# HGRN2 keys as logarithms, clamped sigmoids, one modulation vector fewer, and a plan with more trials, in a two-layer hybrid backbone

## The chip, the cores and the metric

The kernel runs on 1 core of one Trainium2 chip. The metric is the device time of one execution in microseconds (us). The engines of the core run side by side and wait for one another through semaphores: TensorE (PE, matmuls), VectorE (DVE), ScalarE (ACT), GpSimd (POOL) and SyncE (SP, which starts the DMAs here).

## The reference

Two layers work on 256 latent and 256 context tokens of width 1024. What matters here is the HGRN2 mixer, a gated linear recurrence run in both directions over 8 heads of 128 keys, and the modulation that scales and shifts the normalized tokens:

```python
def hgrn2_direction(q, i, z, lb, s0):
    f = lb + (1.0 - lb) * jax.nn.sigmoid(z)
    log_f = jnp.log(jnp.maximum(f, HG_MIN_F))
    k = (1.0 - lb) * jax.nn.sigmoid(-z)
    return hgrn2_chunk_scan(q, k, i, log_f, s0)

# in hgrn2_chunk_scan, per chunk:
    cum = jnp.cumsum(fb, axis=2)
    o_inter = einsum(qb * jnp.exp(cum), state)
    diff = cum[:, :, :, None, :] - cum[:, :, None, :, :]
    scores = einsum('bhtk,bhsk,bhtsk->bhts', qb, kb, exp(diff) where s <= t)
    new_state = state * exp(last) + einsum(kb * jnp.exp(last - cum), vb)

# in reference, per layer:
    need_ctx = l < DEPTH - 1
    sh1, sc1, ga1, sh2, sc2, ga2 = adaln_modulation(c, ...)
    csh1, csc1, cga1, csh2, csc2, cga2 = adaln_modulation(c_ctx, ...)
```

Beside HGRN2 run attention and a long convolution (Hyena); the three are merged with sigmoid gates, projected, and an MLP follows. In layer 1 (the last) the context tokens are only read by the mixers: of their modulation, nothing but the first shift and scale is used. The lower bound `lb` is zero in layer 0.

## The kernel before

All tokens are held with channels on the 128 partitions, 512 tokens (256 latent, 256 context) along the free axis. Every weight block of 128 x 1024 is one *job* in `run_jobs`: a DMA brings `raw`, ACT casts it to `whi`, DVE (for a few blocks POOL) subtracts to get `wlo`, and PE runs three matmuls for each of eight blocks of the inner dimension (high times high and the two cross terms), into the PSUM tile `pd`. A function given with the job then takes the result out of PSUM. In layer 0 most jobs have 512 columns; in layer 1, `q`, the gates, the branches and the MLP have 256.

The HGRN2 jobs of a layer (`hgrn_jobs`) come first. Per head they are the two gate projections `z` (one for each direction), `q` and the output gate, with `v` projected for two heads at a time. `hg_z` turns a `z` of 512 columns into the key `k` and the logarithm of the forget gate `ls`, with `softplus_parts` as its first step: Abs, Exp and Ln on ACT, and min-and-subtract on DVE. `softplus_parts` also serves the output gate (`ev_g`) and the merge gates (`sigmoid`). `hg_scan` then works on one head:

- two prefix sums `cf`, `cb` on DVE;
- per direction the keys decayed to the end of their chunk, `kh`: a subtraction on POOL, an Exp on ACT, a product with `k` on DVE, then transposes (`kt`) and state updates (`pu`, `st`) on PE;
- for four block sizes h = 64, 32, 16, 8 the decayed queries `dq` and keys `dk`: four subtractions on POOL, two Exps on ACT, on DVE one product for `dq` and two half-width products for `dk`, then small matmuls into the scores `sc`;
- inside blocks of 8 the same with `dp`, `dm`; the diagonal with `kd`; then the output `po`, its norm and the gate.

The modulation of layer 1, and part of layer 0's, is worked out on DVE by `ada_vec`: per chunk of 128 channels a DMA of 128 x 1024 (`adav`, in a slot of the `raw` pool), and for each of the two vectors (latent, context) one multiply-and-sum `junk` over 1024 columns. These chunks run as fillers: 40 chunks of layer 1 beside the MLP of layer 0, 8 beside the MLP of layer 1.

The order of all instructions is fixed ahead by a planner. `Plan.record` notes each operation with a cost from `Plan.cost`, its inputs and its priority; `Plan.schedule` simulates five in-order engines and the tile slots (a ring of 63 tiles of 512 columns, 4 `raw`, 4 `whi`, 4 `wlo`, 8 PSUM banks) and picks, for each engine, what can start first. An operation that feeds another engine is assumed to be seen there 60 ns after its end, and 1400 ns (`TLAT`) after it if the other is PE. Between two operations of one engine nothing is added. `Plan.issue` writes the instructions out in that order, so that all of them carry line 433.

Of the kernel before, what the change touches and what calls it, by code (L numbers as in the profile page):

```python
# [22 lines left out]
P = 128  # L23
# [8 lines left out]
MIN_F = 1e-6  # L32
ATT_SCALE = P ** -0.5
# [22 lines left out]
TLAT = 1400.0  # L56
# [91 lines left out]
class Op:  # L148
    __slots__ = ("eng", "calls", "cost", "prio", "succ", "soft", "ndep", "ready", "allocs", "uses", "start", "fin", "seq", "lat", "tail", "lock")
# [7 lines left out]
class Plan:  # L157
# [13 lines left out]
    def cost(self, eng, m, outs, ins, kw):  # L171
# [3 lines left out]
        if eng == "tensor":  # L175
# [3 lines left out]
            if o.shape[0] <= 64:  # L179
                return (45.0 if o.shape[0] > 32 else 50.0 if n >= 128 else 14.0), 165.0, False  # L180
# [35 lines left out]
    def record(self, eng, calls):  # L216
# [9 lines left out]
        for m, a, kw in calls:  # L226
# [4 lines left out]
            c, op.tail, lock = self.cost(eng, m, outs, ins, kw)  # L231
            op.cost += c
# [6 lines left out]
        soft = set()  # L239
        for vt, c in list(rd) + list(wr):  # L240
# [38 lines left out]
    def schedule(self, caps, margin, window):  # L279
        SEM = 60.0  # L280
        lat = {(a, b): 60.0 for a in ENGS for b in ENGS}
        for e in ENGS:
            lat[e, "tensor"] = TLAT
# [44 lines left out]
        while len(order) < total:  # L328
# [127 lines left out]
class Kern:  # L456
# [284 lines left out]
    def ada_vec(self, l, c0, c1):  # L741
        nc = self.nc
        for ch in range(c0, c1):
# [3 lines left out]
            m = self.modb[l][ch // 16][:, ch % 16, :]  # L747
            for v in range(2):
# [1071 lines left out]
```

## Time and profile before

| what | value |
|---|---|
| median of 3 runs | 2187.66 us (2187.34 to 2192.6) |
| the profiled execution | 2191.69 us |
| its span, first to last instruction | 2189.9 us |
| PE busy | 2105.6 us (96%) |
| DVE busy | 1836.8 us (84%) |
| ACT busy | 1201.1 us (55%) |
| POOL busy | 812.8 us (37%) |
| mean granted TensorE clock | 0.984 |

The first layer's HGRN2 lies between about 90 and 430 us, its other mixers and merge up to about 980, its MLP up to about 1300; the second layer's HGRN2 between about 1380 and 1680 us, then its other mixers to about 1850, then merge and MLP. A busy PE is one that has a matmul under way: matmuls overlap, and their ends are modelled. The granted clock is a mean over a stretch of TensorE's two levels, 1.2 GHz (0.5) and 2.4 GHz (1.0).

### The profile page before, as it was taken

What the parts mean: (1) busy time and instruction counts of PE and PEld (TensorE: products, weight loads), DVE (VectorE), ACT (ScalarE), POOL (GpSimd) and SP (SyncE); (2) the same over time, 40 slices, a digit from 0 to 9 for tenths busy, and PEclk for the clock granted to TensorE, in tenths of its full rate; (3) what the DMA queues carried; (4) which work ended last, traced back from release to release, by engine and by line L of the source; (5) the groups of instructions that cost most, each with busy time, mean ns of one, the idle gap of its engine ahead of it and who ended that gap; (6) DMA issues with size and microseconds to landing.
All of it is one profiled execution on the core that took longest, in us unless ns stands there. A gap on an engine that the chain in (4) does not pass through costs nothing.

```text
span 2189.9 us, 38470 instructions
## 1 busy us (share of the span) xinstructions
PE 2105.6 (96%) x14721; PEld 1863.7 (85%) x14721; DVE 1836.8 (84%) x2940; ACT 1201.1 (55%) x2192; POOL 812.8 (37%) x894
## 2 busy tenths in 40 slices
PE   6999999999999999999999989999888999999999
PEld 3888887888888888889888878888778998999999
DVE  8889999998887777788888887899888999668776
ACT  5667757533477534455332334768675458576553
POOL 3565656655430123153100113554645762112110
PEclk9899999999999999999999999999998999999999
DMA  9422222323221454454666654422224433667665
GB/s 331 135 73 78 71 85 69 107 78 97 85 73 52 144 153 154 145 204 128 203 192 194 190 174 154 135 88 78 78 78 154 155 103 95 184 187 211 219 223 154
DMA packets 105608, 301.63 MB, mean 138 GB/s; under 512 B 11456, under 2 KB 26832, under 8 KB 105296
## 3 DMA queue, kind: packets, MB, share of 16 engines
q1 hardware_dynamic: 105424, 299.17, 43.7%
q8 instruction: 116, 1.90, 0.4%
q14 instruction: 68, 0.56, 0.1%
HBM read 281.82 MB, written 14.69 MB: 135 GB/s over the span
## 4 chain that ended last, share of the span: by engine, by line
PE 53%; DVE 27%; DMA 7%; issue 6%; ACT 4%; POOL 2%; SPq 0%; DVEq 0%; POOLq 0%; ACTq 0%
PE pd L433 41%; DMA adav<-in_ada_t 6%; DVE wlo L433 6%; PE pdt L433 4%; DVE junk L433 3%; DVE dk L433 2%; DVE sp L433 1%; ACT sp L433 1%; PE py L433 1%; DVE dq L433 1%; ACT whi L433 1%; PE att L433 1%; PE px L433 1%; DVE hyu L433 1%; DVE mx L433 1%
## 5 line engine op out<-in xcount | busy, mean ns | idle before, releaser
L433 PE MATMUL pd<-hhi,wlo 128*128 128x512 f32 (+2 forms) x1984 | 697.2, 351 | 10.3 <-DVE wlo L433 6.9
L433 PE MATMUL pd<-hlo,whi 128*128 128x512 f32 (+2 forms) x1984 | 683.5, 344 | 0.4 <-DVE hlo L433 0.3
L433 PE MATMUL pd<-hhi,whi 128*128 128x512 f32 (+2 forms) x1984 | 683.4, 344 | 0.0
L433 ACT CAST whi<-raw 128x1024 fp32r<-128x1024 f32 x392 | 409.8, 1047 | 366.8 <-PE pd L433 319.3
L433 DVE TENSOR_TENSOR wlo<-raw,whi 128x1024 fp32r<-128x1024 f32 x376 | 508.8, 1357 | 90.7 <-ACT whi L433 89.8
L433 PEld LDWEIGHTS pd<-hhi,wlo 128*128 128x128 f32 x1984 | 380.8, 192 | 54.3 <-DVE wlo L433 7.1
L433 PEld LDWEIGHTS pd<-hlo,whi 128*128 128x128 f32 x1984 | 380.4, 192 | 45.5 <-DVE hlo L433 1.1
L433 PEld LDWEIGHTS pd<-hhi,whi 128*128 128x128 f32 x1984 | 381.2, 192 | 39.4
L433 DVE SCALAR_TENSOR_TENSOR junk<-adav,crowb 128x1024 bf16<-128x1024 f32 x160 | 205.2, 1299 | 89.4 <-DMA adav<-in_ada_t 87.3
L433 ACT ACTIVATE sp<-sp 128x512 f32<-128x512 f32 (+1 forms) x288 | 160.7, 560 | 71.0 <-DVE sp L433 64.9
L433 POOL TENSOR_TENSOR glo<-relu,ghi 128x512 fp32r<-128x512 f32 (+1 forms) x32 | 46.1, 1440 | 354.2 <-ACT ghi L433 297.7
L433 PE MATMUL pd<-ghi,wlo 128*128 128x256 f32 (+1 forms) x528 | 175.4, 332 | 0.0
L433 PE MATMUL pd<-glo,whi 128*128 128x256 f32 (+1 forms) x528 | 174.9, 331 | 0.0
L433 PE MATMUL pd<-ghi,whi 128*128 128x256 f32 (+1 forms) x528 | 174.8, 331 | 0.0
L433 PE MATMUL pd<-ahi,wlo 128*128 128x512 f32 (+1 forms) x384 | 129.0, 336 | 0.0
L433 PE MATMUL pd<-alo,whi 128*128 128x512 f32 (+1 forms) x384 | 129.0, 336 | 0.0
L433 PE MATMUL pd<-ahi,whi 128*128 128x512 f32 (+1 forms) x384 | 128.9, 336 | 0.0
L433 POOL TENSOR_TENSOR sp<-sp,sp 128x512 f32<-128x512 f32 (+1 forms) x32 | 40.5, 1266 | 208.5 <-DVE sp L433 208.5
L433 PEld LDWEIGHTS pd<-ghi,whi 128*128 128x128 f32 x528 | 100.2, 190 | 9.4
L433 PEld LDWEIGHTS pd<-glo,whi 128*128 128x128 f32 x528 | 100.2, 190 | 9.4
L433 PEld LDWEIGHTS pd<-ghi,wlo 128*128 128x128 f32 x528 | 100.3, 190 | 9.3
L433 ACT CAST ghi<-relu 128x512 fp32r<-128x512 f32 (+1 forms) x64 | 32.9, 514 | 130.9 <-DVE relu L433 126.3
(301 smaller groups left out, 4569.5 us busy)
## 6 DMA issues: line engine op xcount, KB each, us to landing
raw<-in_w_in SPq DMA_DIRECT2D x180, 512.0 KB, 3.7
raw<-in_w_mlp SPq DMA_DIRECT2D x128, 512.0 KB, 4.3
adav<-in_ada_t SPq DMA_DIRECT2D x80, 512.0 KB, 4.2
raw<-in_w_branch SPq DMA_DIRECT2D x48, 512.0 KB, 3.7
raw<-in_w_tm SPq DMA_DIRECT2D x20, 512.0 KB, 3.7
hd<-fhs SPq DMA_DIRECT2D x32, 256.0 KB, 4.0
hf<-hd SPq DMA_DIRECT2D x32, 256.0 KB, 4.8
raw<-in_w_out SPq DMA_DIRECT2D x16, 512.0 KB, 3.7
```

The source lines that it names most:

```text
L433: getattr(eng, m)(*[res(v) for v in a], **{k: res(v) for k, v in kw.items()})
```

## The change

1. *Sigmoids.* `softplus_parts` goes. A new `clamp` bounds `z` to plus or minus 44 on DVE, reading PSUM, and `softplus` makes ln(1 + exp(sign z)) with Exp and Ln on ACT. `hg_z` calls it twice: `lf` is minus the logarithm of sigmoid(z), `nk` minus that of sigmoid(-z). `k` is one Exp of `nk`, in layer 1 with the logarithm of 1 - lb (`lolb`, made once) as the bias. The merge and output gates use the same two functions.
2. *Keys as logarithms.* `hg_scan` makes, for each direction, `g` = prefix sum minus the key's logarithm, on DVE, in the tile of `nk`. The decayed keys `kh` and `dk` are then one exponential of a difference with `g`: for `kh` three activations of 128 columns with a bias (`eb`, a tiny DVE product) in place of a POOL subtraction, one activation and a DVE product; for `dk` the same POOL subtractions and activation, and no DVE product.
3. *Context modulation.* In layer 1 `ada_vec` makes only the latent vector for chunks 16 to 47.
4. *The plan.* Reading what the same engine (other than PE and SP) has just written waits until its end and 40 ns more. Small matmuls cost other amounts, and 186 or 380 ns are added for the first of a group. The assumed latencies to PE (800 to 2600 ns) and to the others (60, 100, 150 ns) are tried in fifteen pairs, and the order that ends first by the planner's own count is taken.

```diff
-TLAT = 1400.0
+TRIALS = [(t, e) for t in (800.0, 1100.0, 1400.0, 1700.0, 2600.0) for e in (60.0, 100.0, 150.0)]
...
             if o.shape[0] <= 64:
-                return (45.0 if o.shape[0] > 32 else 50.0 if n >= 128 else 14.0), 165.0, False
+                return (52.0 if o.shape[0] > 32 else 19.4 if n <= 32 else 12.0 + 0.42 * n), 165.0, False
...
+            if eng == "tensor" and m == "matmul" and outs[0].shape[0] <= 64 and not op.cost:
+                c += 380.0 if outs[0].shape[0] > 32 else 186.0
...
+        op.reads = {vt.writer[c] for vt, c in rd if vt.writer[c] is not None and vt.writer[c].eng == eng}
...
+        found = [(attempt(x)[0], i) for i, x in enumerate(trials)]
+        return attempt(trials[min(found)[1]])[1]
...
-                x.ready = max(x.ready, free_t[e] if x.eng == e and not o.lat else o.fin + lat[e, x.eng])
+                if x.eng != e or o.lat:
+                    t = o.fin + lat[e, x.eng]
+                else:
+                    t = o.fin + RAW if o in x.reads and e not in ("tensor", "sync") else free_t[e]
+                x.ready = max(x.ready, t)
...
+            nv = 1 if l == DEPTH - 1 and ch >= 16 else 2
+            m = self.modb[l][ch // 16][:, ch % 16, 0:nv]
-            for v in range(2):
+            for v in range(nv):
...
-    def softplus_parts(self, z, n):
+    def clamp(self, z, n):
+        t = self.T("zc")[:, :n]
+        self.nc.vector.tensor_scalar(out=t, in0=z, scalar1=-ZCAP, scalar2=ZCAP, op0=ALU.max, op1=ALU.min)
+        return t
+
+    def softplus(self, z, n, sign):
         nc = self.nc
         t = self.T("sp")[:, :n]
-        nc.scalar.activation(out=t, in_=z, func=AF.Abs)
-        nc.scalar.activation(out=t, in_=t, func=AF.Exp, scale=-1.0)
+        nc.scalar.activation(out=t, in_=z, func=AF.Exp, scale=sign)
         nc.scalar.activation(out=t, in_=t, func=AF.Ln, bias=1.0)
-        nc.vector.scalar_tensor_tensor(out=t, in0=z, scalar=0.0, in1=t, op0=ALU.min, op1=ALU.subtract)
         return t
...
     def hg_z(self, l, dr, hd, z):
-        ls = self.softplus_parts(z, 512)
+        z = self.clamp(z, 512)
+        lf = self.softplus(z, 512, -1.0)
+        nk = self.softplus(z, 512, 1.0)
         k = self.T("hk")
-        nc.vector.tensor_tensor(out=k, in0=ls, in1=z, op=ALU.subtract)
-        nc.scalar.activation(out=k, in_=k, func=AF.Exp)
         if l == 0:
-            nc.vector.tensor_scalar(out=ls, in0=ls, scalar1=math.log(MIN_F), scalar2=None, op0=ALU.max)
+            nc.scalar.activation(out=k, in_=nk, func=AF.Exp, scale=-1.0)
+            nc.vector.tensor_scalar(out=lf, in0=lf, scalar1=-math.log(MIN_F), scalar2=None, op0=ALU.min)
         else:
...
+            nc.scalar.activation(out=k, in_=nk, func=AF.Exp, scale=-1.0, bias=self.lolb[:, i:i + 1])
...
-            nc.vector.tensor_scalar(out=k, in0=k, scalar1=self.olb[:, i:i + 1], scalar2=None, op0=ALU.mult)
-        return k, ls
+        return k, lf, nk
...
+        gf, gb = nkf, nkb
+        for d, (g_, c_) in enumerate(((gf, cf), (gb, cb))):
+            if l == 0:
+                V.tensor_tensor(out=g_, in0=c_, in1=g_, op=ALU.subtract)
+            else:
+                i = d * 8 + hd
+                V.scalar_tensor_tensor(out=g_, in0=g_, scalar=self.lolb[:, i:i + 1], in1=c_, op0=ALU.subtract, op1=ALU.add)
...
-            e = ch(c_)[:, :, last:last + 1]
-            G.tensor_tensor(out=ch(kh), in0=ch(c_), in1=e.to_broadcast([P, 4, P]), op=ALU.subtract)
-            A.activation(out=kh, in_=kh, func=AF.Exp, scale=-1.0)
-            V.tensor_tensor(out=kh, in0=kh, in1=k_, op=ALU.mult)
+            e = ch(c_)[:, :, last:last + 1].rearrange("p c o -> p (c o)")
...
+            el = self.S([P, 4], "eb")
+            V.tensor_scalar(out=el, in0=e, scalar1=sg, scalar2=None, op0=ALU.mult)
+            for c in order:
+                sl = slice(c * P, (c + 1) * P)
+                A.activation(out=kh[:, sl], in_=g_[:, sl], func=AF.Exp, scale=-sg, bias=el[:, c:c + 1])
...
-            G.tensor_tensor(out=bl(dk)[:, :, :h], in0=cfb[:, :, :h], in1=rf, op=ALU.subtract)
-            G.tensor_tensor(out=bl(dk)[:, :, h:], in0=cbb[:, :, h:], in1=rb, op=ALU.subtract)
+            G.tensor_tensor(out=bl(dk)[:, :, :h], in0=bl(gf)[:, :, :h], in1=rf, op=ALU.subtract)
+            G.tensor_tensor(out=bl(dk)[:, :, h:], in0=bl(gb)[:, :, h:], in1=rb, op=ALU.subtract)
...
-            V.tensor_tensor(out=bl(dk)[:, :, :h], in0=bl(dk)[:, :, :h], in1=bl(kf)[:, :, :h], op=ALU.mult)
-            V.tensor_tensor(out=bl(dk)[:, :, h:], in0=bl(dk)[:, :, h:], in1=bl(kb)[:, :, h:], op=ALU.mult)
...
-        order = self.plan.schedule(CAPS, MARGIN, WINDOW)
+        order = self.plan.best_schedule(CAPS, MARGIN, WINDOW, TRIALS)
```

## Rows read from the trace of the kernel before

**Rows 1.** The page: span, and busy us of each engine.
```profile
span 2189.9 us, 38470 instructions
PE 2105.6 (96%) x14721; PEld 1863.7 (85%) x14721; DVE 1836.8 (84%) x2940; ACT 1201.1 (55%) x2192; POOL 812.8 (37%) x894
```

**Rows 2.** Busy time by stretch: length, engines' busy us, clock, DMA share, GB/s.
```profile
0.00:100.00 100.00, 77.41 (x518) 61.30 (x519) 88.55 (x176) 56.62 (x104) 43.48 (x40) 0.91 0.67 237
100.00:450.00 350.00, 341.11 (x3161) 286.96 (x3160) 325.11 (x447) 229.94 (x415) 213.01 (x243) 1.00 0.27 82
...
700.00:1300.00 600.00, 599.64 (x2838) 504.06 (x2837) 474.90 (x714) 243.43 (x363) 117.61 (x83) 1.00 0.54 169
1300.00:1380.00 80.00, 71.64 (x396) 62.10 (x395) 63.54 (x93) 37.85 (x63) 34.03 (x31) 0.96 0.42 135
1380.00:1700.00 320.00, 286.79 (x2553) 261.39 (x2552) 282.50 (x490) 215.28 (x470) 172.83 (x262) 0.94 0.34 105
1700.00:1850.00 150.00, 144.31 (x1068) 136.58 (x1068) 142.00 (x253) 92.93 (x197) 78.43 (x74) 0.99 0.38 115
1850.00:2189.90 339.90, 335.60 (x2776) 334.24 (x2774) 245.83 (x399) 191.49 (x322) 53.80 (x50) 1.00 0.64 194
```

**Rows 3.** PE's waits, 1380 to 1700 us: total us, times, longest.
```profile
PE sc L433 <- DVE dm L433: 13.5, 6, 4.8
PE pd L433 <- DVE wlo L433: 5.9, 4, 2.4
PE po L433 <- DVE am L433: 4.3, 1, 4.3
PE kt L433 <- DVE kh L433: 3.5, 1, 3.5
```

**Rows 4.** DVE's groups by form: shapes, count, busy us, mean ns, idle before.
```profile
L433 DVE SCALAR_TENSOR_TENSOR junk<-adav,crowb 128x1024 bf16<-128x1024 f32 x160 | 205.2, 1299 | 89.4 <-DMA adav<-in_ada_t 87.3 <-issue 2.1
L433 DVE SCALAR_TENSOR_TENSOR sp<-pd,sp 128x512 f32<-128x512 f32 x64 | 43.8, 685 | 12.1 <-ACT sp L433 11.9
L433 DVE TENSOR_TENSOR dk<-dk,hk 128x256 f32<-128x256 f32 x64 | 40.0, 665 | 2.5 <-ACT dk L433 2.4
L433 DVE TENSOR_TENSOR kh<-kh,hk 128x512 f32<-128x512 f32 x32 | 28.0, 886 | 1.0 <-ACT kh L433 0.8
L433 DVE TENSOR_TENSOR dk<-dk,hk 128x128 f32<-128x128 f32 x64 | 25.3, 429 | 1.8 <-ACT dk L433 1.6
L433 DVE TENSOR_TENSOR hk<-sp,pd 128x512 f32<-128x512 f32 x32 | 21.9, 686 | 0.9
L433 DVE TENSOR_SCALAR sp<-sp 128x512 f32<-128x512 f32 x32 | 17.3, 541 | 0.9
L433 DVE TENSOR_SCALAR hk<-hk,olb 128x512 f32<-128x512 f32 x16 | 9.1, 566 | 1.2 <-ACT hk L433 1.2
L433 DVE TENSOR_SCALAR mx<-mx 128x1 f32<-128x1 f32 x48 | 7.0, 151 | 1.0
```

**Rows 5.** ACT's groups by form.
```profile
L433 ACT ACTIVATE sp<-sp 128x512 f32<-128x512 f32 x192 | 120.8, 631 | 59.0 <-DVE sp L433 55.1
L433 ACT ACTIVATE sp<-sp 128x256 f32<-128x256 f32 x96 | 40.1, 418 | 12.0 <-DVE sp L433 9.8
L433 ACT ACTIVATE sp<-pd 128x512 f32<-128x512 f32 x64 | 37.7, 589 | 4.3 <-PE pd L433 4.1
L433 ACT ACTIVATE relu<-relu,w1b 128x256 f32<-128x256 f32 x32 | 16.2, 507 | 3.2 <-DVE relu L433 3.1
```

**Rows 6.** POOL's groups by form: the removed subtraction, one of its two kinds.
```profile
L433 POOL TENSOR_TENSOR kh<-cf 128x512 f32<-128x512 f32 x16 | 23.1, 1444 | 16.8 <-DVE cf L433 16.8
```

**Rows 7.** DVE's groups, 1400 to 1700 us: the weights' low part.
```profile
L433 DVE TENSOR_TENSOR wlo<-raw,whi 128x1024 fp32r<-128x1024 f32 x39 | 57.7, 1483 | 6.4 <-ACT whi L433 6.0
```

**Rows 8.** DVE's timeline, 1604 to 1640 us: start, us, instruction.
```profile
1609.96 4.22 DVE L433 TENSOR_TENSOR wlo<-raw,whi 128x1024 fp32r<-128x1024 f32 x1
...
1633.46 1.21 DVE L433 TENSOR_TENSOR wlo<-raw,whi 128x1024 fp32r<-128x1024 f32 x1
```

More of the change, by code (lines that the diff above doesn't have):

```diff
@@ L148 @@
 class Op:
-    __slots__ = ("eng", "calls", "cost", "prio", "succ", "soft", "ndep", "ready", "allocs", "uses", "start", "fin", "seq", "lat", "tail", "lock")
+    __slots__ = ("eng", "calls", "cost", "prio", "succ", "soft", "ndep", "ready", "allocs", "uses", "start", "fin", "seq", "lat", "tail", "lock", "reads")
 ENGS = ("tensor", "vector", "scalar", "gpsimd", "sync")
@@ L277, in record, with best_schedule, attempt, schedule @@
         return op
-    def schedule(self, caps, margin, window):
-        SEM = 60.0
-        lat = {(a, b): 60.0 for a in ENGS for b in ENGS}
+    def best_schedule(self, caps, margin, window, trials):
+        ndep = [o.ndep for o in self.ops]
+        vts = list({id(v): (v, v.left) for o in self.ops for v in o.uses}.values())
+        def attempt(x):
+            for o, n in zip(self.ops, ndep):
+                o.ndep, o.ready = n, 0.0
+            for v, n in vts:
+                v.left, v.slot, v.end = n, None, 0.0
+            try:
+                order = self.schedule(caps, margin, window, *x)
+            except RuntimeError:
+                return 1e12, None
+            return max(o.fin for o in order), order
+        found = [(attempt(x)[0], i) for i, x in enumerate(trials)]
+        return attempt(trials[min(found)[1]])[1]
+    def schedule(self, caps, margin, window, tlat, elat):
+        SEM, RAW = 60.0, 40.0
+        lat = {(a, b): elat for a in ENGS for b in ENGS}
         for e in ENGS:
-            lat[e, "tensor"] = TLAT
+            lat[e, "tensor"] = tlat
         lock_t, lock_e = 0.0, None
@@ L754, in ada_vec @@
                 if chunk <= ch < chunk + 8:
-                    nc.vector.tensor_scalar(out=self.amod[l][which][:, ch - chunk, :], in0=m, scalar1=1.0,
+                    nc.vector.tensor_scalar(out=self.amod[l][which][:, ch - chunk, 0:nv], in0=m, scalar1=1.0,
                                             scalar2=self.pv(g, l * 8 + ch - chunk), op0=ALU.add, op1=ALU.mult)
@@ L1223, in hg_scan @@
         for c_ in (cf, cb):
-            A.activation(out=c_[:, :nq], in_=c_[:, :nq], func=AF.Exp)
+            A.activation(out=c_[:, :nq], in_=c_[:, :nq], func=AF.Exp, scale=sg)
             V.tensor_tensor(out=c_[:, :nq], in0=c_[:, :nq], in1=q[:, :nq], op=ALU.mult)
@@ L1263, in ev_z @@
                     s = st[hd]
[L1264 removed]
+                    d = "fb"[dr]
+                    s["k" + d], s["l" + d], s["nk" + d] = self.hg_z(l, dr, hd, z)
                 def ev_q(z, hd=hd):
@@ L1271, in ev_g @@
                 def ev_g(z, hd=hd):
-                    t = self.softplus_parts(z, nq)
-                    nc.scalar.activation(out=t, in_=t, func=AF.Exp)
+                    t = self.sigmoid(z, nq)
                     nc.vector.tensor_tensor(out=t, in0=t, in1=z, op=ALU.mult)
@@ L1493, in sigmoid @@
     def sigmoid(self, z, n):
-        t = self.softplus_parts(z, n)
-        self.nc.scalar.activation(out=t, in_=t, func=AF.Exp)
+        t = self.softplus(self.clamp(z, n), n, -1.0)
+        self.nc.scalar.activation(out=t, in_=t, func=AF.Exp, scale=-1.0)
         return t
```

34 lines of the change are left out of this document (19 added, 15 removed).

## The prediction

> **What bounds the kernel now.** Read the page from the top. TensorE (PE) is busy for 96% of the span, VectorE (DVE) for 84% [rows 1]. A PE that is busy all the time can't be helped by work taken from DVE, so the next question is where the missing 4% lies, and the view that answers it is the busy time by stretch [rows 2]. From 700 to 1300 us PE is busy 599.64 of 600 us: there TensorE alone sets the time, and nothing that the change does to other engines can shorten it; its matmuls are the same before and after. The same holds from 1850 us on, where 335.60 of 339.90 us are busy and the rest is the tail.
>
> The loss is in four other stretches, and the granted clock belongs to it: in 1380 to 1700 us PE is idle for 320 - 286.8 = 33.2 us, and the clock is 0.94 on average, so that of the two levels, 1.2 and 2.4 GHz, it spent about 12% at the lower one, worth up to 0.06 x 320 = 19.2 us of full-speed work. Together 52.4 us. The same sum gives 11.6 us for 1300 to 1380 (8.4 idle, 3.2 clock), 7.2 us for 1700 to 1850 (5.7 and 1.5), and 8.9 us, all of it idle, for 100 to 450 us [rows 2]. That is 80.1 us which the change could reach at most; it is an upper bound, since idle time and low clock overlap in part. The first 100 us lose 31.6 us more (22.6 idle, 9 clock), but in start-up work that the change hardly touches.
>
> 1380 to 1700 us is the HGRN2 mixer of the second layer. There DVE is busy 282.5 of 320 us (88%), while ScalarE (ACT) has 215.3 and GpSimd (POOL) 172.8 [rows 2], and the waits of PE name DVE: the scores' matmuls wait 13.5 us for `dm`, the projections 5.9 us for `wlo` [rows 3]. So in this stretch DVE's queue is what ends last. The first layer's mixer (100 to 450) has DVE at 325.1 of 350 us, and yet PE at 97.5%: its jobs are 512 columns wide, so PE has more to do for the same DVE work. These two stretches are where the change removes DVE work.
>
> **Part by part: DVE.** Durations are means of one instruction in the profiled execution.
> - *Sigmoid parts* (`hg_z`). Before, each of 16 calls per layer made on DVE the min-and-subtract from PSUM (685 ns), `k = ls - z` (686), the bound on the logarithm (541), and in layer 1 also scaling and `k` times `olb` (566) [rows 4]. After, a clamp reading PSUM takes the place of the first, and `k` comes from ACT alone. The trace has no clamp; the rows bound it by 541 ns (a two-scalar operation from SBUF) and 685 (a PSUM read of the same width), and I take 685, as it reads PSUM. So 0.69 us less per call in layer 0, 11 us in all, and 0.69 + 0.57 = 1.25 us less in layer 1, 20 us in all.
> - *Scan.* Per head two `kh` products (886 each) go, and eight `dk` products (665 each at 256 columns in layer 0, 429 each at 128 in layer 1). Added are two operations `g = c - nk` with two SBUF inputs over 512 columns, for which I take the 886 of `kh`, and two tiny scalings (151, the row of `mx`) [rows 4]. Layer 0: 1.77 + 5.32 - 1.77 - 0.30 = 5.0 us a head, 40 us for eight. Layer 1: 1.77 + 3.43 - 1.77 - 0.30 = 3.1 us, 25 us for eight.
> - *Modulation of context.* 32 of layer 1's 48 chunks lose one of two `junk` products of 1.30 us [rows 4]: 24 before 1300 us (31 us of DVE), 8 in the last MLP (10 us).
>
> So DVE falls by about 51 us of 325 in the first mixer, by 45 us of 282 in the second, by 31 us ahead of 1300 us. The last lies where PE is full, so by itself it is hidden at no gain; it can only let the filter units and the normalization at 1300 us come earlier.
>
> **POOL and ACT.** POOL loses two `kh` subtractions a head, 1.44 us each [rows 6]: some 20 us of its 173 in the second mixer. This helps DVE twice over, since DVE's times there swing with what runs beside it: one `wlo` took 4.22 us and another 1.21 us [rows 8]. The 39 `wlo` of this stage average 1.48 us [rows 7], 0.27 above that 1.21, 11 us in all beside 173 us of POOL work; an eighth of POOL's work goes, so 1.3 us, and as `wlo` is a fifth of DVE's time here I count four times that, 5 us; bounds 0 and 20 us (all of POOL's time).
>
> ACT gains work. Each `hg_z` has one activation more (631 instead of an Abs at 589 plus 631 new: 0.67 us), so 10.7 us per layer. `kh` becomes three activations of 128 columns with a bias from memory in place of one of 512 at about 0.63 us. From 631 at 512 and 418 at 256 columns the fixed part is 205 ns, so 128 columns cost 311; a pointer adds 507 - 418 = 89; together 400 each, 1.2 us for three, at most 0.57 more per `kh`, and 9 us for the sixteen of a layer. The output gate's sigmoid gives back one activation a head (5 us and 3 us) [rows 5]. ACT in the second mixer goes from 215 to about 232 us, still beside DVE's work. The last `eb` and `el` operations are on the path of `kh`, but a POOL pass of 1.4 us and a DVE product go out of the same path, so it gets shorter.
>
> A rule of the Trainium skill (ScalarE: Activation LUTs, What ACT_TABLE_LOAD costs) speaks against that split: it gives an activation with a pointer bias 280 ns + 0.833 ns per column, an immediate one 186 ns + 0.833 ns, and an overlap of 93 ns back to back. By it, as an estimate, three pieces cost 3 x 294 = 881 ns of throughput against 520, or 5.8 us per layer instead of my 9. Rows 5 agree with the pointer's price (89 ns against 93). The sum by it would be 3 us of ACT time smaller, which changes no term on the path.
>
> **The new plan.** Three things change in the order itself: a wait of 40 ns behind each read-after-write on one engine, dearer small matmuls, and fifteen trials of assumed latencies, of which the one that finishes first by its own arithmetic is taken. The trace of before can't show that order. Its bounds from the rows: at best PE gets all of the 80 us back; at worst the first mixer loses PE time at the rate at which the second does now, 350 x (0.104 + 0.06) - 8.9 = +48 us [rows 2]. I take zero for the order itself, because the other mixer's 2.5% loss shows that an order with long assumed PE latency already hides nearly everything when DVE keeps up.
>
> **The sum.** Second mixer: DVE needs 282.5 - 45 - 5 = 232 us, while PE needs 320 - 52 = 268. DVE's share would be 87%, below the 93% with which the first mixer lost 2.5%. So most of the 52.4 us should come back; I take 40, since the jobs here are short and waits on single heads stay. First mixer: 5 of 8.9. 1300 to 1380: 6 of 11.6, from the 31 us of DVE that go ahead of it. 1700 to 1850: 3 of 7.2, since the attention there is not touched. Start: 0. Together 54 us. The profiled execution took 2191.69 us (span 2189.9, 1.8 around it); it would become 2137.7. The median of the three timed runs is 2187.66, 4 us lower, and gives 2134.
>
> **The rivals.**
> 1. *ACT takes DVE's place.* With 232 us of ACT work and in-order queues, a stage of 270 us has ACT at 86% and DVE at 86%. Two full queues that wait on each other (`sp`, `hk` go back and forth) lose more than one. For it: ACT is the engine that grows. Against it: ACT idles a third of that stage now. It would return half, 27 us: 2161.
> 2. *All of the loss returns.* Shorter waits also keep the clock at its upper level, which has cost up to 19 us in the second mixer; then 80 us come back: 2108.
> 3. *PE's loss is not DVE's work but the heads' dependence.* The single-head chain of scan, exponentials, scores and output ends late whatever DVE's load is. Then only the shorter path of `kh` pays: 1.44 + 0.89 - 0.89 - 0.57 = 0.9 us per pass, of which PE waited for 3.5 us in the second mixer [rows 3]: 2184, no change that a measurement can tell. Against it: that stage's DVE is never idle for long.
> 4. *The plan turns against it.* The trial chosen by its own finish favours short assumed latencies, since the latency is part of that finish. PE's order is fixed; with operands planned closer, it stands in front of late ones in both mixers. From the point on where the first mixer's loss grows by more than the second one's gain the kernel is slower. At the second mixer's present rate in the first (+48) and nothing gained in the second: 2236; half of it: 2212.
> 5. *More live tiles.* Two more 512-column tiles live per head from the projection to the scores, in a ring of 63. If the ring runs out, allocation holds back the next head. I put it with rival 1, as it has the same place and size.
>
> **Chances.** Forecast (2120 to 2160) 0.50; rival 1 and 5 (2160 to 2181) 0.20; rival 2 (below 2120) 0.12; rival 3 0.08; rival 4 0.10. About 0.3%, 6.6 us, is what a measurement of this kernel can tell from no change; so faster 0.82, same 0.08, slower 0.10. Range 2100 to 2180: it takes in rival 1 and nearly all of rival 2, and leaves out rivals 3 and 4, 0.18.
>
> **What would show it.** Right: in the stretch between the second layer's first and last HGRN2 projections PE idles under 15 us, its clock stays at 0.98 or more, and DVE's busy time falls by some 45 us there; the waits of the scores on `dm` shrink; the stretch of 600 us of full PE keeps its length. DVE's sum over the span should be about 140 us lower, POOL's 45 lower, ACT's within 20 us of before. Wrong: DVE falls so, and PE's idle time doesn't, with ACT or a single head's chain at the end of its waits (rivals 1, 3), or PE idles in the first mixer where it did not (rival 4).

## The result, and the profile after

| what | before | after |
|---|---|---|
| median | 2187.5 us (2185.86 to 2192.6) | 2123.89 us (2121.76 to 2124.91) |
| the profiled execution | 2191.69 us | 2123.79 us |
| its span | 2189.9 us | 2121.6 us |

The ratio after to before is 0.9706, with a 95% interval of 0.969 to 0.9722: 63.6 us less. The forecast was 2134, in a range of 2100 to 2180.

The head of the page, which answers [rows 1]: span, then busy time, share of the span and instructions of each engine; below it the granted clock in 40 slices, and the shares of the chain that ended last.

```profile
span 2121.6 us, 38292 instructions
PE 2085.7 (98%) x14721; PEld 1847.3 (87%) x14721; DVE 1674.8 (79%) x2733; ACT 1187.6 (56%) x2225; POOL 785.0 (37%) x862
PEclk9999999999999999999999999999999999999999
PE 85%; DVE 8%; ACT 4%; DMA 1%; issue 1%; SPq 0%; POOL 0%; ACTq 0%; DVEq 0%
```

DVE lost 162 us, POOL 28, ACT 13.5. PE's idle time fell from 84.3 us (2189.9 - 2105.6) to 35.9 (2121.6 - 2085.7). That is 48.4 of the 68.3 us by which the profiled span is shorter; the other 19.9 are PE's own busy time for the same 14721 matmuls, and the mean granted clock went from 0.984 to 0.996. The chain that ended last is PE for 85% of the span.

To see where the time went, the two traces must be cut at the same work, since the second mixer of after begins 24 us earlier. The cuts here are the starts of the same projection matmuls (the n-th of the program in both). Busy time by stretch, columns as in [rows 2]; first the stretches of before that [rows 2] cuts elsewhere:

```profile
0.00:80.00 80.00, 57.41 (x374) 42.46 (x375) 70.61 (x140) 42.98 (x77) 37.89 (x37) 0.89 0.73 262
80.00:450.10 370.10, 361.21 (x3305) 305.90 (x3305) 343.14 (x483) 243.58 (x441) 218.70 (x247) 1.00 0.28 85
450.10:980.30 530.20, 529.31 (x2688) 449.88 (x2686) 423.71 (x669) 269.21 (x466) 170.98 (x161) 1.00 0.39 120
980.30:1300.10 319.80, 319.44 (x1574) 271.27 (x1574) 265.57 (x421) 107.78 (x158) 46.20 (x37) 1.00 0.58 181
...
1700.00:2189.90 489.90, 479.90 (x3842) 470.82 (x3841) 387.83 (x650) 284.41 (x518) 132.23 (x124) 1.00 0.56 170
```

and then the same work in after, all seven stretches:

```profile
0.00:70.50 70.50, 53.33 (x349) 36.50 (x350) 59.31 (x130) 38.10 (x68) 33.95 (x35) 0.93 0.78 284
70.50:445.90 375.40, 374.33 (x3437) 320.18 (x3435) 311.78 (x460) 257.78 (x502) 220.93 (x254) 1.00 0.29 89
445.90:962.20 516.30, 516.30 (x2585) 438.18 (x2582) 399.10 (x639) 249.55 (x434) 153.50 (x139) 1.00 0.39 121
962.20:1283.00 320.80, 319.90 (x1575) 271.21 (x1575) 248.26 (x385) 113.51 (x166) 59.19 (x42) 1.00 0.59 186
1283.00:1355.60 72.60, 70.67 (x404) 61.87 (x403) 54.68 (x82) 34.52 (x58) 30.61 (x28) 1.00 0.45 149
1355.60:1643.50 287.90, 282.10 (x2620) 257.75 (x2619) 236.56 (x427) 222.64 (x517) 166.20 (x254) 0.99 0.36 115
1643.50:2121.60 478.10, 469.10 (x3766) 461.56 (x3764) 365.09 (x616) 271.51 (x486) 120.66 (x113) 1.00 0.55 171
```

The second mixer (320 us in [rows 2], 287.9 here) gave 32.1 us, the start 9.5, the first mixer with what follows it 8.6 (5.3 longer and 13.9 shorter: 132 matmuls more lie in the former, 103 fewer in the latter), 1300 to 1380 gave 7.3 and the rest 11.8. The cuts don't part PE's work quite the same way: 25 matmuls fewer lie in the start, 67 more in the second mixer, 76 fewer behind it. So neighbouring stretches are best read together. The 320 us of full PE from 980 on kept their length (+1.0). In the second mixer PE idles 5.8 us instead of 33.2, at a clock of 0.99 instead of 0.94, with 45.9 us less of DVE. PE's waits there (total us, times, longest), to be set beside [rows 3]:

```profile
PE pd L460 <- DVE wlo L460: 2.9, 1, 2.9
PE pu L460 <- ACT kts L460: 1.3, 2, 0.7
PE pdt L460 <- ACT hhi L460: 0.7, 1, 0.7
PE oss L460 <- POOL csl L460: 0.4, 1, 0.4
PE kt L460 <- ACT kh L460: 0.2, 1, 0.2
```

The 13.5 us for `dm` are gone, and so are those for `am` and for `kh` of DVE. What ACT took over is hardly waited for: 2.2 us in all.

The new instructions, by form (count, busy us, mean ns, idle before), beside [rows 4] and [rows 5]:

```profile
L460 DVE TENSOR_SCALAR zc<-pd 128x512 f32<-128x512 f32 x64 | 43.7, 683 | 21.8 <-PE pd L460 21.4
...
L460 DVE TENSOR_SCALAR eb<-cb 128x4 f32<-128x4 f32 x16 | 10.5, 658 | 0.0
...
L460 DVE SCALAR_TENSOR_TENSOR sp<-sp,lolb,cb 128x512 f32<-128x512 f32 x8 | 8.2, 1025 | 0.0
...
L460 DVE TENSOR_TENSOR sp<-cb,sp 128x512 f32<-128x512 f32 x8 | 6.1, 757 | 0.4
...
L460 DVE TENSOR_SCALAR eb<-cf 128x4 f32<-128x4 f32 x16 | 5.0, 315 | 0.0
...
L460 ACT ACTIVATE kh<-sp,eb 128x128 f32<-128x128 f32 x96 | 33.1, 392 | 27.0 <-DVE eb L460 26.8
...
L460 ACT ACTIVATE hk<-sp,lolb 128x512 f32<-128x512 f32 x16 | 11.4, 715 | 0.0
L460 ACT ACTIVATE hk<-sp 128x512 f32<-128x512 f32 x16 | 10.1, 631 | 0.3
```

### The profile page after: what moved, and what is told of

Read it like the earlier page. It is cut to its first block, busy times and chain, and to the rows that moved or that the text cites. A ratio compares the mean times of both kernels' runs of the same rounds, so it can differ in the third digit from the quotient of the medians.

```text
span 2121.6 us, 38292 instructions
## 1 busy us (share of the span) xinstructions
PE 2085.7 (98%) x14721; PEld 1847.3 (87%) x14721; DVE 1674.8 (79%) x2733; ACT 1187.6 (56%) x2225; POOL 785.0 (37%) x862
## 4 chain that ended last, share of the span: by engine, by line
PE 85%; DVE 8%; ACT 4%; DMA 1%; issue 1%; SPq 0%; POOL 0%; ACTq 0%; DVEq 0%
PE pd L460 68%; PE pdt L460 4%; PE py L460 2%; PE px L460 1%; DVE wlo L460 1%; PE sco L460 1%; PE att L460 1%; PE sc L460 1%; PE po L460 1%; ACT sp L460 1%; DVE y L460 1%; PE pu L460 1%; PE ptr L460 1%; ACT whi L460 1%; DVE hlo L460 1%
## 5 line engine op out<-in xcount | busy, mean ns | idle before, releaser
L460 ACT CAST whi<-raw 128x1024 fp32r<-128x1024 f32 x392 | 410.8, 1049 | 540.1 <-PE pd L460 487.9
L460 PE MATMUL pd<-hhi,wlo 128*128 128x512 f32 (+2 forms) x1984 | 689.8, 348 | 4.5 <-DVE wlo L460 4.5
L460 DVE TENSOR_TENSOR wlo<-raw,whi 128x1024 fp32r<-128x1024 f32 x376 | 499.1, 1329 | 104.1 <-ACT whi L460 103.0
L460 PEld LDWEIGHTS pd<-hhi,whi 128*128 128x128 f32 x1984 | 376.9, 190 | 39.2
L460 DVE SCALAR_TENSOR_TENSOR junk<-adav,crowb 128x1024 bf16<-128x1024 f32 x128 | 165.4, 1310 | 76.8 <-DMA adav<-in_ada_t 76.7
L460 ACT ACTIVATE sp<-sp 128x512 f32<-128x512 f32 (+1 forms) x224 | 122.4, 566 | 3.0 <-DVE sp L460 0.7
L460 POOL TENSOR_TENSOR pa<-pa,pb 128x256 f32<-128x256 f32 x96 | 79.7, 863 | 76.8 <-DVE pb L460 69.5
```

The costliest lines, as they stand in the source:

```text
L460: getattr(eng, m)(*[res(v) for v in a], **{k: res(v) for k, v in kw.items()})
```

## The experiments

Ratios are to the kernel before, timed beside each on the same chip; "against after" is the difference of the two ratios times 2187.5 us.

| kernel | what it is | median us | ratio [95%] | against after |
|---|---|---|---|---|
| after | | 2123.89 | 0.9706 [0.969, 0.9722] | |
| e1_plan_only | arithmetic of before, new plan | 2173.85 | 0.9929 [0.9912, 0.9945] | +48.8 |
| e2_math_only | arithmetic of after, old plan | 2147.60 | 0.9808 [0.9793, 0.9822] | +22.3 |
| e3_ctx_back | both modulation vectors | 2131.97 | 0.9736 [0.9721, 0.9751] | +6.6 |
| e4_keys_back | keys as products | 2153.83 | 0.9836 [0.9822, 0.9851] | +28.4 |
| e5_dve_load | 8 products more a head | 2136.23 | 0.9764 [0.975, 0.9779] | +12.7 |
| e6_old_costs | old costs of small matmuls | 2135.28 | 0.9758 [0.9743, 0.9772] | +11.4 |
| e7_no_raw | no same-engine wait | 2127.52 | 0.9723 [0.9708, 0.9738] | +3.7 |
| e8_1700_60 | one fixed pair of latencies | 2122.02 | 0.9699 [0.9683, 0.9715] | -1.5 |
| e9_dve_pool_load | e5 and 2 POOL passes a head | 2152.20 | 0.9835 [0.9821, 0.985] | +28.2 |
| e10_trials_only | only the trials of the new plan | 2136.42 | 0.9755 [0.9737, 0.9772] | +10.7 |
| e11_wide_trials | 48 other pairs | 2134.56 | 0.9751 [0.9735, 0.9768] | +9.8 |
| e12_sigm_back | old sigmoid parts | 2122.64 | 0.9697 [0.9682, 0.9711] | -2.0 |

Lengths of the seven stretches, in us, cut at the same matmuls in the profile of each kernel (4 of the 12 in full, the others where they are used):

| kernel | start | first mixer | to 980 | to 1300 | to 1380 | second mixer | rest |
|---|---|---|---|---|---|---|---|
| before | 80.0 | 370.1 | 530.2 | 319.8 | 79.9 | 320.0 | 489.9 |
| after | 70.4 | 375.4 | 516.3 | 320.8 | 72.7 | 287.9 | 478.1 |
| e1_plan_only | 69.4 | 388.4 | 522.4 | 321.1 | 77.1 | 306.7 | 485.3 |
| e2_math_only | 79.6 | 369.3 | 518.2 | 319.9 | 69.1 | 304.4 | 485.9 |
| e4_keys_back | 70.5 | 387.7 | 523.7 | 320.5 | 72.5 | 292.3 | 484.8 |
| e9_dve_pool_load | 70.2 | 378.2 | 526.2 | 320.0 | 72.5 | 299.7 | 483.2 |

**Plan or arithmetic.** The theory was that the arithmetic brings nearly everything and the order nothing. Two kernels each take one half.

e1_plan_only, before with the planner of after:

```diff
-TLAT = 1400.0
+TRIALS = [(t, e) for t in (800.0, 1100.0, 1400.0, 1700.0, 2600.0) for e in (60.0, 100.0, 150.0)]
...
-        order = self.plan.schedule(CAPS, MARGIN, WINDOW)
+        order = self.plan.best_schedule(CAPS, MARGIN, WINDOW, TRIALS)
```

> The kernel before with the new planner alone: its costs, the 40 ns behind a read of what the same engine wrote, and the fifteen trials; no arithmetic is changed, so DVE keeps its 1837 us of work. Theory A (the time came from DVE's work, the order is worth nothing by itself): within 10 us of the kernel before, 2178 to 2197. Theory B (the order is what gained; the lighter DVE only rode along): at least half of the 64 us, 2155 or below. Theory C (an order planned with shorter assumed latency is worse where DVE is still full): 2200 or above.

e2_math_only, after with the planner of before:

```diff
-TRIALS = [(t, e) for t in (800.0, 1100.0, 1400.0, 1700.0, 2600.0) for e in (60.0, 100.0, 150.0)]
+TLAT = 1400.0
...
-        order = self.plan.best_schedule(CAPS, MARGIN, WINDOW, TRIALS)
+        order = self.plan.schedule(CAPS, MARGIN, WINDOW)
```

> The changed arithmetic (sigmoids, keys as logarithms, one modulation vector fewer) under the old planner: old costs, 1400 ns to PE, 60 ns elsewhere, one trial. Theory A: nearly all of the gain, 2120 to 2140, with the second mixer's PE idle time below 15 us. Theory B: less than half of it, 2156 or above, with DVE lower by some 140 us all the same.

Measured 2173.85 and 2147.60. Both fell between the theories: the plan alone brings 2187.5 x (1 - 0.9929) = 15.5 us, the arithmetic alone 2187.5 x (1 - 0.9808) = 42.0, and the plan brings 22.3 more on top of the new arithmetic. So the order isn't worth zero. Busy time by stretch of the second mixer, e1_plan_only first and then e2_math_only:

```profile
1378.30:1685.10 306.80, 283.44 (x2557) 257.07 (x2556) 277.98 (x490) 213.41 (x470) 180.37 (x259) 0.97 0.33 105
```

```profile
1356.10:1660.60 304.50, 286.97 (x2598) 260.97 (x2597) 240.57 (x421) 232.17 (x517) 160.49 (x252) 0.97 0.36 115
```

In e2_math_only DVE is down by 41.9 us, and yet PE still idles for 304.5 - 287.0 = 17.5 us. PE's waits there, in e2_math_only:

```profile
PE sc L435 <- ACT whi L435: 4.5, 2, 3.2
PE pu L435 <- ACT kts L435: 3.2, 4, 1.3
PE pd L435 <- DVE cm L435: 3.2, 1, 3.2
PE pd L435 <- DVE wlo L435: 2.3, 1, 2.3
PE kt L435 <- ACT kh L435: 1.3, 2, 0.7
```

With the four smaller waits that follow, ACT is the name beside 9.0 us and DVE beside 8.4; before, over the same stretch, it was 1.2 and 31.8. So under the old order the place that DVE left was taken in part by ACT, which is the first rival in part; under the new order it isn't (2.2 us).

The new order alone helps and hurts. In e1_plan_only the start is 10.6 us shorter and the second mixer 13.3, but in the first mixer, with DVE's old work, PE idles 388.4 - 372.4 = 16.0 us, where before has 8.9, and its wait for `kh` of DVE is 11.1 us instead of 3.2:

```profile
69.40:457.80 388.40, 372.36 (x3389) 316.24 (x3388) 365.00 (x510) 248.06 (x459) 229.43 (x262) 0.99 0.27 85
```

**Context modulation.** e3_ctx_back:

```diff
-            nv = 1 if l == DEPTH - 1 and ch >= 16 else 2
+            nv = 2
```

> The changed kernel with both modulation vectors made again for layer 1's chunks 16 to 47: 32 more products on DVE, 42 us by their 1.31 us. Theory A as put in the prediction (this part lies where PE is full and is hidden): 0 to 6 us slower than the changed kernel, 2124 to 2130, with the loss, if any, about 1300 us. Theory B' (DVE's queue ahead of the second layer sets that layer's start, so that the 31 us before it count in good part): 15 us or more slower, 2139 or above.

Measured 2131.97, 6.6 us over after and between the two theories; all other stretches are within 1.4 us of after, and 1300 to 1380 is 82.5 us instead of 72.7. Busy time and PE's largest wait in that stretch of e3_ctx_back:

```profile
1283.60:1366.10 82.50, 74.67 (x405) 63.97 (x404) 62.43 (x93) 38.36 (x64) 36.19 (x33) 0.96 0.45 153
```

```profile
PE fsum L460 <- POOL ffb L460: 5.9, 3, 3.6
```

Here `ffb` and `fsum` are tiles of the convolution's filters, and POOL makes this `ffb` from one that DVE made. Before has the same wait in its 1300 to 1380 us, and after has none:

```profile
PE fsum L433 <- POOL ffb L433: 8.2, 2, 6.4
```

So the 31 us of DVE ahead of 1300 cost nothing where they lie (to 1300: 320.8 in both) and 10 us where they end. The total moved by 6.6, less than the stretch: the rest is within what the median and one profiled execution of this kernel differ by (2131.97 and 2135.16).

**The keys.** e4_keys_back puts the scan of before into after: POOL subtraction, one activation and a DVE product for `kh`, and products for `dk`:

```diff
-                A.activation(out=kh[:, sl], in_=g_[:, sl], func=AF.Exp, scale=-sg, bias=el[:, c:c + 1])
+            G.tensor_tensor(out=ch(kh), in0=ch(c_), in1=e.to_broadcast([P, 4, P]), op=ALU.subtract)
+            A.activation(out=kh, in_=kh, func=AF.Exp, scale=-1.0)
+            V.tensor_tensor(out=kh, in0=kh, in1=k_, op=ALU.mult)
...
+            V.tensor_tensor(out=bl(dk)[:, :, :h], in0=bl(dk)[:, :, :h], in1=bl(kf)[:, :, :h], op=ALU.mult)
+            V.tensor_tensor(out=bl(dk)[:, :, h:], in0=bl(dk)[:, :, h:], in1=bl(kb)[:, :, h:], op=ALU.mult)
```

> The changed kernel with the scan of before: kh and dk are multiplied by the key again, g is not made; sigmoids, modulation and planner stay changed. This gives DVE back some 65 us (40 in the first mixer, 25 in the second) and POOL 45 us. Theory A: 15 to 30 us slower than the changed kernel, 2139 to 2154, most of it in the second mixer. Theory B (the order gained): within 8 us of the changed kernel, 2116 to 2132. Rival on ACT (the changed scan moves the bound to ACT, so that giving ACT its work back helps as much as DVE's work hurts): also within 8 us, with ACT's share at the end of PE's waits smaller than after.

Measured 2153.83, +28.4: as expected, and the largest single part. But e4_keys_back changes three things: the load of DVE, the load of POOL, and the length of the path to `kh`. Two kernels add loads to after and leave its path alone; what they add is read by nobody, though it takes tiles of the ring.

e5_dve_load, the DVE products only:

```diff
+            spare = self.T("spare")
+            V.tensor_tensor(out=bl(spare)[:, :, :h], in0=bl(dk)[:, :, :h], in1=bl(kf)[:, :, :h], op=ALU.mult)
+            V.tensor_tensor(out=bl(spare)[:, :, h:], in0=bl(dk)[:, :, h:], in1=bl(kb)[:, :, h:], op=ALU.mult)
```

> The changed kernel with eight more DVE products per head, as wide as the dk products that were removed, written to a tile that nobody reads: 40 us of DVE work in the first mixer and 25 us in the second come back, and the planner knows of them, but nothing waits for them and no path gets longer; POOL and ACT are as after the change. Theory A1 (the amount of work on DVE's queue is what cost the time): 20 to 30 us slower than the changed kernel, about what putting the keys' products back cost (28 us), 2144 to 2154. Theory A2 (the shorter path from scan to scores gained, not the load): within 6 us of the changed kernel, 2118 to 2130. Between the two: load explains half.

e9_dve_pool_load, the same and in each direction one subtraction on POOL:

```diff
+            spare = self.T("sparep")
+            G.tensor_tensor(out=ch(spare), in0=ch(c_), in1=ch(c_)[:, :, last:last + 1].to_broadcast([P, 4, P]), op=ALU.subtract)
```

> The kernel with the eight unread DVE products per head (13 us slower than the changed kernel), and with two unread POOL subtractions per head of 512 columns on top, as long as those that the change took away (45 us of POOL over both layers). Putting the whole scan of before back cost 28 us, so 15 us are left to explain. If POOL's work is what they are (its use of the port that DVE's two-input operations share, or its own queue): 2144 to 2154. If they are the longer path from scan to scores and to kh, which this kernel does not have: within 4 us of the kernel with DVE products alone, 2132 to 2140.

Measured +12.7 for DVE alone, between the two theories, and +28.2 with POOL: 15.5 more, and as much in all as e4_keys_back (+28.4). The heads of the three pages, e4_keys_back, e5_dve_load and e9_dve_pool_load:

```profile
PE 2094.8 (97%) x14721; PEld 1851.2 (86%) x14721; DVE 1768.1 (82%) x2829; ACT 1183.3 (55%) x2161; POOL 825.0 (38%) x894
```

```profile
PE 2088.1 (98%) x14721; PEld 1847.4 (87%) x14721; DVE 1729.4 (81%) x2861; ACT 1190.0 (56%) x2225; POOL 778.4 (36%) x862
```

```profile
PE 2092.6 (97%) x14721; PEld 1849.9 (86%) x14721; DVE 1762.9 (82%) x2861; ACT 1191.5 (55%) x2225; POOL 819.8 (38%) x894
```

The loads of e9_dve_pool_load are within 6 us of those of e4_keys_back on DVE and on POOL, and loads of this size suffice for the whole loss. But it isn't shown that the shorter path brings nothing, for PE's waits differ between the two kernels. Over the span, e4_keys_back:

```profile
PE kt L460 <- DVE kh L460: 10.5, 9, 3.2
PE sc L460 <- DVE dk L460: 5.8, 8, 2.1
```

and e9_dve_pool_load:

```profile
PE kt L460 <- ACT kh L460: 6.8, 7, 1.5
PE pd L460 <- POOL wlo L460: 5.2, 2, 4.6
PE sc L460 <- ACT dk L460: 1.0, 1, 1.0
```

So `kh` and `dk`, the end of that path, are waited for longer in e4_keys_back, and in e9_dve_pool_load a part of the loss is POOL's own queue (0.2 us for that `wlo` in e4_keys_back, 2.2 in e5_dve_load).

DVE has the same 2861 instructions in e5_dve_load and e9_dve_pool_load, and took 33.5 us longer beside 41.4 us more of POOL. A single form of instruction can't show whether POOL is the cause. The product `dm` doubles from e5_dve_load to e9_dve_pool_load, while the clamp `zc`, which reads PSUM, stays; but `dm` is as long in e6_old_costs (below), where POOL has no instruction more and only the order differs:

```profile
L460 DVE TENSOR_TENSOR dm<-dm,hk 128x256 f32<-128x256 f32 x16 | 6.9, 430 | 0.0
L460 DVE TENSOR_SCALAR zc<-pd 128x256 f32<-128x256 f32 x32 | 13.5, 421 | 5.4 <-PE pd L460 5.0
```

```profile
L460 DVE TENSOR_TENSOR dm<-dm,hk 128x256 f32<-128x256 f32 x16 | 13.6, 850 | 0.1
L460 DVE TENSOR_SCALAR zc<-pd 128x256 f32<-128x256 f32 x32 | 13.4, 419 | 9.8 <-PE pd L460 9.5
```

```profile
L458 DVE TENSOR_TENSOR dm<-dm,hk 128x256 f32<-128x256 f32 x16 | 14.1, 882 | 0.8 <-ACT dm L458 0.8
```

The sum over all forms can show it. 2212 instructions of DVE are the same in all fourteen kernels of this document, as many of each form. Their durations added up, in us, least and most among the kernels:

| what the DVE instruction reads | count | the ten kernels with 862 POOL instructions | the four with 894 (before, e1, e4, e9) |
|---|---|---|---|
| PSUM | 848 | 417.9 to 419.7 | 418.4 to 419.1 |
| two tensors in SBUF | 1049 | 981.3 to 1001.6 | 1012.0 to 1029.7 |
| one tensor in SBUF | 315 | 107.2 to 115.6 | 114.2 to 120.4 |

The order alone moves the second row by up to 20 us, but the 32 POOL subtractions move it further: in that row no kernel of one group lies in the range of the other, and e5_dve_load, with more work on DVE alone, stays in the lower one (982.2). The Trainium skill (GPSIMD Engine Reference, 1. Specifications) says that POOL shares its SBUF interfaces with VectorE, and that instructions of VectorE with two SBUF inputs are among those that contend; the second row agrees.

By stretch the agreement of e9_dve_pool_load and e4_keys_back is rougher: over after, e4_keys_back loses 19.8 us up to 980 and 11.1 from 1380 on, e9_dve_pool_load 12.5 and 16.9. And in e5_dve_load the second mixer took 285.6 us, no more than in after, though DVE was busy 247.4 us there instead of 236.6; its loss lies in the first mixer (386.7). So it is the total that the loads match, not each stretch.

**The sigmoids.** e12_sigm_back brings back `softplus_parts` (in the gates too) and makes the key's logarithm on DVE:

```diff
-        z = self.clamp(z, 512)
-        lf = self.softplus(z, 512, -1.0)
-        nk = self.softplus(z, 512, 1.0)
+        lf = self.softplus_parts(z, 512)
+        nk = self.T("nk")
+        nc.vector.tensor_tensor(out=nk, in0=z, in1=lf, op=ALU.subtract)
```

> The changed kernel with the sigmoid parts of before (Abs, Exp, Ln, and min-and-subtract on DVE) and nk made from them by one more DVE subtraction reading PSUM; keys as logarithms, modulation and planner stay changed. DVE has 0.69 us more per call, 11 us per layer, ACT one activation less per call, and PSUM is held until both reads are done. By DVE's load alone, at the 13 us for 67 us of unread products: 4 us slower, 2126 to 2131. If holding PSUM longer costs PE its banks: 2134 or above. If ACT is the tight engine: no slower or faster, 2124 or below.

Measured 2122.64: no difference to after (the intervals overlap), with DVE at 1686.0 us (+11.2) and ACT at 1194.2 (+6.6). That the sigmoids bring anything isn't shown. That ACT was the tight one, which a low time was to mean, isn't shown either, since ACT got no less work here.

**The parts of the plan.** e6_old_costs takes back the new costs of small matmuls:

```diff
-                return (52.0 if o.shape[0] > 32 else 19.4 if n <= 32 else 12.0 + 0.42 * n), 165.0, False
+                return (45.0 if o.shape[0] > 32 else 50.0 if n >= 128 else 14.0), 165.0, False
...
-            if eng == "tensor" and m == "matmul" and outs[0].shape[0] <= 64 and not op.cost:
-                c += 380.0 if outs[0].shape[0] > 32 else 186.0
```

> The changed kernel, planned with the old costs of small matmuls (no 186 or 380 ns for the first of a group); the 40 ns rule and the fifteen trials stay. If the costs carry the plan's 23 us: 2140 or above. If the latency or the 40 ns rule carries them: 2118 to 2130.

e7_no_raw takes back the wait behind a read-after-write on one engine:

```diff
-                    t = o.fin + RAW if o in x.reads and e not in ("tensor", "sync") else free_t[e]
+                    t = free_t[e]
```

> The changed kernel, planned without the wait behind a read on the same engine; costs and trials stay (the trial taken becomes 1100 and 150 ns). If the rule carries the plan's 23 us: 2140 or above. If it is the latencies or the costs: 2118 to 2130.

e10_trials_only takes back both:

> The changed arithmetic under the old costs and without the 40 ns rule, but with the fifteen trials (800 and 100 ns are taken). Against the old planner's 1400 and 60 ns (2148 for the same arithmetic): if the choice of the latency carries the part of the plan's gain that costs (11 us) and rule (4 us) leave, 2136 to 2142. If trials are worth nothing without the truer costs: 2144 to 2152.

Measured 2135.28, 2127.52 and 2136.42. The costs have a place of their own: the start. It takes 81.4 us in e6_old_costs and 86.6 in e10_trials_only, 80.0 in before and 79.6 in e2_math_only, the four with the old costs; in after and the nine kernels with the new ones it takes 68.1 to 71.8. The +10.9 us of e6_old_costs there are nearly its whole +11.4. That is half of the plan's 22.3, between what the two theories gave. Busy time from 40 to 60 us, after and then e6_old_costs:

```profile
40.00:60.00 20.00, 18.37 (x144) 15.13 (x143) 18.15 (x40) 12.65 (x24) 12.93 (x16) 0.83 0.61 219
```

```profile
40.00:60.00 20.00, 12.02 (x96) 8.85 (x96) 19.86 (x36) 5.69 (x12) 10.22 (x11) 0.83 0.51 180
```

PE gets 18.4 us of work in where the old costs let it have 12.0. In the whole start the filters' matmuls wait 5.8 us for `fr` and 4.9 for `fsl` of DVE in e6_old_costs, and 0.2 for `fsl` in after. The same-engine wait makes no difference that these runs can tell (e7_no_raw +3.7, intervals overlapping). The trials by themselves, which take 800 and 100 ns, take the second mixer from 304.4 us (e2_math_only) to 292.8 (e10_trials_only), PE's idle time there from 17.5 to 8.7, and the whole from 2147.60 to 2136.42.

**How well the planner chooses.** The trials take the pair whose order ends first by the planner's count. e8_1700_60 gives it one other pair, e11_wide_trials a choice of 48:

```diff
-TRIALS = [(t, e) for t in (800.0, 1100.0, 1400.0, 1700.0, 2600.0) for e in (60.0, 100.0, 150.0)]
+TRIALS = [(1700.0, 60.0)]
```

> The changed kernel with one trial alone, 1700 ns to PE and 60 ns elsewhere, in place of the 800 and 150 ns that it takes; by the planner's own count this order ends 1.7 us later. If the choice among trials carries the plan's gain, through the latencies: 2140 or above, near the old planner's 2148 for the same arithmetic. If the rules carry it and the latencies matter little: 2118 to 2132.

```diff
-TRIALS = [(t, e) for t in (800.0, 1100.0, 1400.0, 1700.0, 2600.0) for e in (60.0, 100.0, 150.0)]
+TRIALS = [(t, e) for t in (300.0, 500.0, 650.0, 800.0, 950.0, 1250.0, 1550.0, 2000.0) for e in (80.0, 120.0, 150.0, 180.0, 220.0, 300.0)]
```

> The changed kernel with 48 trials in place of fifteen, from 300 to 2000 ns and from 80 to 300 ns; 500 and 80 ns are taken, which by the planner's count end 2.7 us earlier than the changed kernel's 800 and 150. If the planner's count says what the chip does, 2119 to 2123. If the count is blind at this size (the order that counted 1.7 us later ran 1.5 us faster): anywhere from 2115 to 2135.

| kernel | pair taken (ns) | the planner's count | measured |
|---|---|---|---|
| e8_1700_60 | 1700, 60 | 2084.6 us | 2122.02 us |
| after | 800, 150 | 2083.0 us | 2123.89 us |
| e11_wide_trials | 500, 80 | 2080.2 us | 2134.56 us |

So with the new costs and the wait, a pair near the old 1400 and 60 has all of the plan's gain (e8_1700_60), and another loses half of it (e11_wide_trials); without them a pair brings half (e10_trials_only). The parts don't add up.

The order that counts best ran worst. Among orders this close the count is blind, and one and the same arithmetic under the same rules ran anywhere in 12.5 us. That is a yardstick for all the runs above, for each edit makes a new order: a difference of the whole below some 13 us isn't settled by the median alone, and three orders may not show the whole of it. The distances of e1, e2, e4 and e9 to after are above it; the 15.5 us of the plan in e1 and of POOL between e5 and e9 hardly. e3, e6 and e10 are below it and rest on their one stretch; e5, e7 and e12 stay open at their size. No kernel here beats after: e8_1700_60 and e12_sigm_back tie with it.

## Why the prediction held, and which step of it did not

**The total.** The point was 2134 and the time 2123.89, inside the forecast's own range of 2120 to 2160. But the sum came out right in part because two errors cancelled. All 54 us were put down to the arithmetic, which alone brings 42.0; nothing was put down to the order, which brings 22.3 on top.

**The step that failed** is "I take zero for the order itself, because the other mixer's 2.5% loss shows that an order with long assumed PE latency already hides nearly everything when DVE keeps up". e2_math_only has that order and a DVE at 79% of the second mixer, below the first mixer's 93%, and PE still lost 17.5 us of 304.5 there. In the first mixer the step held: PE idles 0.35 us there, less than in after (1.1).

```profile
79.60:448.90 369.30, 368.95 (x3407) 316.51 (x3406) 305.35 (x449) 259.37 (x492) 206.30 (x252) 1.00 0.28 88
```

The inference went from that mixer to another with shorter jobs, and left out that waits on ACT come up as those on DVE go (1.2 us before, 9.0 in e2_math_only). Whether the shorter jobs are the reason isn't shown. The bounds that the prediction wrote beside the zero (a gain of up to 80, a loss of up to 48) did hold both values.

**Where DVE's work went** was right in the main: 162 us (about 140 forecast), in the second mixer 45.9 (some 45), and the waits on `dm` are gone. In the first mixer it was 31.4 instead of 51, with 24.6 more in the stretch behind, where the cuts don't part the work alike. The prices: the clamp 683 ns (685 taken), a piece of `kh` 392 (400), `g` 757 to 1025 (886); the bias from memory costs 715 - 631 = 84 ns (89). Only `eb` was off, at 315 and 658 ns on average instead of the 151 of `mx`: 15.5 us in all instead of 4.8. As a price the 151 was right: 13 of the 32 took 156 to 165 ns. The other 19 lasted until just behind the end of a POOL instruction (last section).

**The second mixer and what follows.** Forecast 43 us from 1380 on (40 and 3), measured 32.1 + 11.8 = 43.9; the split differs in part because 67 matmuls moved ahead of the cut. PE idles 5.8 us (under 15 forecast) at a clock of 0.99 (0.98 or more). Of the 43.9 us, 28.4 are idle time that went and 15.5 a shorter busy time of PE for nearly the same matmuls (6395 and 6386) at the higher clock, so both of the prediction's terms, wait and clock, are there. It takes both halves of the change: with the old order 15.6 + 4.0 = 19.6 us, 23 less than the arithmetic was credited with.

**The first mixer** was taken at 5 us of 8.9. With the stretch behind it, it gave 8.6, all of it idle time.

**POOL** was mis-sized twice, and the two errors cancelled. I gave a fall of POOL's work in the second mixer 5 us of DVE, 0.25 us per us of some 20. e9_dve_pool_load against e5_dve_load shows 33.5 us of DVE for 41.4 of POOL over the span, 0.8 per us. But between the cuts POOL fell there by 6.6 us only (172.8 to 166.2), which at 0.8 is 5.3 us. Over the span it fell by 27.8 us instead of 45: the subtractions are gone, but what is left takes longer in this order (785.0 us for the 862 instructions that take 749.9 in e2_math_only).

**1300 to 1380** gave 7.3 us (6 forecast), for the reason given: e3_ctx_back shows the removed products hidden where PE is full, and the wait for `ffb` come back at their end. The stretch to 1300 kept its length to 1.0 us.

**The start** was taken at 0 and gave 9.5, of which 5.4 are idle time of PE. The reason given was that the change hardly touches "start-up work"; its operations are the same, but their order isn't, and e6_old_costs shows that the costs the plan gives to small matmuls set it.

**The rivals.** 1 (ACT takes DVE's place) fell for the whole kernel: ACT is busy 222.6 of 287.9 us, 77%, and PE waits 2.2 us for it; with the old order it was there in part. 2 (all the loss returns, 2108) did not come whole: of the 80 us of its four stretches some 60 came back, and the start, which it had left out, gave the rest of the 68.3 us of the profiled span. 3 (a single head's chain, no gain from DVE's load) fell: unread loads alone cost as much as the keys had gained (e9_dve_pool_load), though a part for the path stays open. 4 (the plan turns against it) fell as to its sign, 22.3 us gained. Its mechanism, PE in front of late operands, shows where DVE kept its old work, in the first mixer of e1_plan_only, with 7 us more of idle time and not 48; and what it argued from, that the planner's own finish is a poor judge, shows in e11_wide_trials, at 11 us. 5 (more live tiles) was not tested by itself.

## What to carry to other kernels

Work taken from the engine that ends last pays only as far as the order of the queues lets the next one move up: time the new work under the old order and the old work under the new one before crediting either. Where one engine's work stretches another's, as POOL's did DVE's here, it counts beyond the waits on its own queue; and a mean duration from one order is no price, so look at the shortest and at what ran beside the long ones. A planner that ranks orders by its own count is worth its costs being measured (here the start), but can't choose among orders that count within a few us of each other.

## What the runs showed of the hardware that was not expected

- POOL's work stretches DVE's, by 0.8 us per us in the one pair of kernels that differ in this and in the order alone: 41.4 us more of POOL made the same 2861 DVE instructions 33.5 us longer. What reads PSUM isn't touched: 848 such instructions took 417.9 to 419.7 us in all fourteen kernels.
- A DVE instruction can last until a POOL instruction ends. The tiny `eb`, on four columns, took 156 to 165 ns in 13 of 32 cases in after. The other 19, of 255 to 2365 ns, all began while a POOL instruction ran and ended 24 to 29 ns after one ended. The longest two began behind a `wlo` of POOL; one of them, in the timelines of DVE and POOL (start, us):

```profile
1500.75 2.36 DVE L460 TENSOR_SCALAR eb<-cb 128x4 f32<-128x4 f32 x1
```

```profile
1500.47 2.61 POOL L460 TENSOR_TENSOR wlo<-raw,whi 128x1024 fp32r<-128x1024 f32 x1
```

So the mean of 658 ns for `eb` from `cb` belongs to the order of after: the same 16 instructions average 207 ns in e5_dve_load and 410 in e8_1700_60.
